# Attention probabilities turned in 32 × 32 squares on VectorE and exchanged through DRAM, instead of transposed on TensorE, in a two-layer diffusion backbone

## The chip, the cores and the metric

The kernel runs on one core of one Trainium2 chip. The metric is the device time of one execution in microseconds (us). Three runs of the kernel before took 1686.21, 1686.81 and 1686.99 us, so its median is 1686.81 us.

## What is computed

Two layers run over 1024 latent tokens of width 1024; 256 context tokens feed the first layer only. Each layer adds a gated branch to x, and a final RMSNorm follows. Layer 0 is windowed attention with 16 query heads, 4 key/value heads, a head size of 128, a window of 128 keys to either side, all 256 context keys and a learned sink in the same softmax. Layer 1 is a Conformer convolution block. What the change touches is the attention:

```python
s_win = jnp.einsum('bqhgd,bkhd->bhgqk', qblk, kw) * scale      # 128 queries, up to 3 blocks of 128 keys
s_win = jnp.where(mask, s_win, -jnp.inf)
s_ctx = jnp.einsum('bqhgd,bchd->bhgqc', qblk, kc) * scale      # 256 context keys
p_ctx, p_win = sink_softmax(sink_l, s_ctx, s_win)
o = (jnp.einsum('bhgqc,bchd->bqhgd', p_ctx, vc)
     + jnp.einsum('bhgqk,bkhd->bqhgd', p_win, vw))
...
y = (o * jax.nn.silu(z)) @ w_out
x = x + gate * y
```

All of it is float32. A product is made of three TensorE matmuls on operands that were split into a high and a low part (high·high, low·high, high·low).

## The kernel before, in words

**Order of the work.** The program is written for the Tile layer, whose scheduler places every engine's instructions by its own simulated times. An engine for which `pin` (line 106) is on keeps the order in which the program names its instructions instead (class InOrder, lines 76 to 91). Since that helper issues everything, all rows of the profile show its line, L89, and one goes by the names of tiles. From line 1260 on, `pin("P")` holds: TensorE works in written order, and VectorE, ScalarE, GpSimd and the SyncE queue (SP), which issues most DMAs, in the scheduler's order.

**The attention loop** (line 1280) has 128 steps, one per head h and block qb of 128 queries. A step writes, for TensorE:

- `scores` (line 1083) of the *next* step: six matmuls into a `pss` bank. VectorE then takes the masked and scaled scores into a page `p_page` with their row minimum, ScalarE takes the exponential, VectorE the reciprocal of the sum, and GpSimd (POOL) multiplies the page by it. `p` then holds 128 queries × 640 keys (512 for the first and the last block of a head): up to five squares of 128 × 128.
- `fill(12)` (line 1070): twelve matmuls of 512 columns out of a queue of projections of later heads (`psg`).
- `pv` (line 1153), the product of probabilities and values into a `pso` bank, when one is due: once per four blocks, 32 times in all; for every other head `pv_shared` (line 1181) adds six short matmuls.
- `transposes` (line 1119) of *this* step's p: five (or four) TensorE transposes into another `pss` bank, from which ScalarE copies the high part `pthi` and VectorE subtracts it for the low part `ptlo`. `pv` reads both. A `pv` is queued at the end of the step whose split closes its four blocks, and runs in the next step behind the fill.

Beside the loop run side works that the loop only advances: `ada_rest` (line 665) loads pieces of 128 KB of the modulation weights (`dww_raw`, `wsum_raw`), which VectorE adds up in `pso`; `low_parts` (line 724) makes the low parts of the two output weights (`low_page`) and stores them in DRAM (`wolA`, `wolC`); the rotary step sends halves through DRAM on ScalarE's queue (`rope_half`); finished heads go to DRAM (`ozd`).

**The output product of layer 1** (`proj_out`, line 1796) runs four passes of eight steps: two token halves, each with two halves of the columns. A step is 24 matmuls of 512 columns, and `ahead` loads the weights (`wo`, `wol`) two steps ahead. At the end of a pass `evac1` (line 1719) runs for each of four row blocks: it names the load of the residual rows (`xr`), adds them, and in the passes for the second column half it also normalises and names the two stores to `out`.

Of the kernel before, what the change touches and what calls it, by code (L numbers as in the profile page):

```python
# [9 lines left out]
F32 = mybir.dt.float32  # L10
# [84 lines left out]
def backbone_kernel(  # L95
# [1023 lines left out]
    def transposes(h, qb):  # L1119
        p = ptile.pop((h, qb))  # L1120
        k0, k1 = max(qb - 1, 0), min(qb + 1, TB - 1)
        nb = k1 - k0 + 1
        tb = ps_s()
        ql = qb % 4
# [7 lines left out]
        tv = tb[:, 0:640].rearrange("p (a b) -> p a b", b=P)  # L1132
        a0, a1 = int(qb == TB - 1), 4 if qb == 0 else 5
        runs = [(a0, a1, slice(ql + 4 * a0, ql + 4 * a1 - 3, 4))]
        if h % 2 == 0 and qb == 3:
            runs = [(1, 5, slice(7, 20, 4)), (0, 1, slice(20, 21))]
        elif h % 2 == 0 and qb == 4:
            runs = [(0, 4, slice(0, 13, 4)), (4, 5, slice(21, 22))]
        for r0, r1, bs in runs:
            anchor_a[:] = [act(pthi[:, bs], tv[:, r0:r1], AF.Copy)]  # L1140
        for r0, r1, bs in runs:
            anchor[:] = [split_lo(V, ptlo[:, bs], tv[:, r0:r1], pthi[:, bs])]

    shared = []

    def pv_mm(o, work):
        for n, (a, b, ps_, os_) in enumerate(work):
            last = n == len(work) - 1
            PE.matmul(o[:, os_], a, pthi[:, ps_], start=n == 0, stop=False)
            PE.matmul(o[:, os_], a, ptlo[:, ps_], start=False, stop=False)  # L1150
            PE.matmul(o[:, os_], b, pthi[:, ps_], start=False, stop=last)

    def pv(h, half):
# [5 lines left out]
        work = [(*(c[:, n, i * P:i * P + P] for n in (2, 3)), slice(4 + 8 * i, 8 + 8 * i), slice(0, 512)) for i in range(2)]  # L1159
        for kb in range(q0, q0 + 4):  # L1160
            qa, qz = max(kb - 1, q0), min(kb + 1, q0 + 3)
            b0 = qa - q0 + 8 * (qa - kb + 1)
            work.append((vh[:, kb], vl[:, kb], slice(b0, b0 + 9 * (qz - qa) + 1, 9), slice((qa - q0) * P, (qz - q0 + 1) * P)))
# [812 lines left out]
```

## Time and profile before

| what | value |
| --- | --- |
| median of three runs | 1686.81 us |
| span of the profiled execution | 1684.8 us |
| between the two | 2.0 us |
| TensorE busy | 1675.0 us, 8436 matmuls |
| VectorE, ScalarE, GpSimd busy | 1116.1, 878.8, 871.0 us |
| DMA | 244.55 MB, mean 145 GB/s |
| attention loop, about | 150 to 750 us of the span |

A row of the timeline gives start and duration in us, the engine, the operation, and the tiles as out<-in; x5 is five instructions with one form in a row. A matmul's printed duration contains the time that it takes to drain, in which the next one already runs, so a matmul's price is the distance between starts. A row of the groups gives count, busy time, mean ns of one, and the idle time before them with what ended it. SPq rows are DMA issues on SP's queue: their duration is that of the issue, not of the transfer. "us to landing" is the median from issue to landing.

### The profile page before, as it was taken

Reading aid. Unit: us, or ns where it says so; the run is one execution under the profiler, and the core shown is the slowest. Engines: PE = TensorE matmul, PEld = TensorE weight load, DVE = VectorE, ACT = ScalarE, POOL = GpSimd, SP = SyncE. Lnnn points to the kernel's source line nnn. Section 1 sums busy time; section 2 is a strip of 40 time slices with the busy share of each in tenths; the row PEclk is TensorE's granted clock in tenths of the full one; section 3 lists DMA queues with packets and bytes.
Section 4 is the critical chain, followed back from the end, with each engine's and each line's share of the span. In section 5 each row is a group of like instructions: output and inputs, shape, how many; then the busy total and the mean of one; then the engine's idle time right before and its main releaser. Section 6 shows DMA issues by size and latency. Waiting matters only on the chain.

```text
span 1684.8 us, 23963 instructions
## 1 busy us (share of the span) xinstructions
PE 1675.0 (99%) x8436; PEld 1413.9 (84%) x8436; DVE 1116.1 (66%) x2131; ACT 878.8 (52%) x1555; POOL 871.0 (52%) x722
## 2 busy tenths in 40 slices
PE   9999999999999999999999999999999999999998
PEld 6888888888888888888888888888888888888886
DVE  5765654566356644566324289999999999868732
ACT  5745543555355543556334365555665654566741
POOL 0256653666366663653001267999898888130400
PEclk9999999999999999999999999999999999999999
DMA  9424443454244443447976522020211202387881
GB/s 387 150 85 153 134 121 95 153 153 141 84 152 144 143 135 98 135 135 251 320 233 228 213 94 91 11 72 17 75 51 51 82 33 80 130 276 241 310 298 50
DMA packets 114776, 244.55 MB, mean 145 GB/s; under 512 B 11626, under 2 KB 36514, under 8 KB 114656
## 3 DMA queue, kind: packets, MB, share of 16 engines
q1 hardware_dynamic: 108576, 233.06, 40.9%
q10 hardware_dynamic: 6080, 9.97, 2.4%
q8 instruction: 66, 1.08, 0.3%
q14 instruction: 54, 0.44, 0.1%
HBM read 190.80 MB, written 41.69 MB: 138 GB/s over the span
## 4 chain that ended last, share of the span: by engine, by line
PE 98%; DVE 0%; DMA 0%; ACT 0%; POOL 0%; issue 0%; ACTq 0%; POOLq 0%
PE psg L89 51%; PE pss L89 26%; PE pso L89 22%; DMA rope_half<-rope_half 0%; POOL rope_half L89 0%; DVE x_page L89 0%; ACT p_page L89 0%; DVE wlo_page L89 0%; ACT pthi L89 0%; ACT rope_half L89 0%; ACT whi_page L89 0%; DVE hf_page L89 0%; DVE hl_page L89 0%; ACT qh_page L89 0%; ACT lhi_page L89 0%
## 5 line engine op out<-in xcount | busy, mean ns | idle before, releaser
L89 POOL TENSOR_TENSOR odd_half<-odd_half,prod_half 128x513 f32<-128x513 f32 (+2 forms) x252 | 314.7, 1257 | 22.6 <-ACT prod_half L89 9.4
L89 POOL TENSOR_TENSOR wlo_page<-wraw_page,whi_page 128x512 fp32r<-128x512 f32 (+1 forms) x104 | 173.0, 1680 | 186.7 <-DVE ql_page L89 72.0
L89 PE MATMUL psg<-hh_page,whi_page 128*128 128x512 f32 x600 | 236.3, 394 | 0.0
L89 PE MATMUL psg<-hl_page,whi_page 128*128 128x512 f32 x600 | 234.4, 391 | 0.0
L89 PE MATMUL psg<-hh_page,wlo_page 128*128 128x512 f32 x600 | 234.0, 390 | 0.0
L89 ACT ACTIVATE prod_half<-ubuf,dww 128x513 f32<-128x513 f32 (+2 forms) x252 | 165.6, 675 | 116.9 <-POOL odd_half L89 113.0
L89 PE MATMUL psg<-h2h_page,whi_page 128*128 128x512 f32 x464 | 181.9, 392 | 0.0
L89 PE MATMUL psg<-h2h_page,wlo_page 128*128 128x512 f32 x464 | 180.6, 389 | 0.0
L89 PE MATMUL psg<-h2l_page,whi_page 128*128 128x512 f32 x464 | 180.6, 389 | 0.0
L89 POOL TENSOR_SCALAR p_page<-p_page,sc 128x640 f32<-128x640 f32 (+1 forms) x128 | 99.6, 779 | 149.5 <-DVE sc L89 131.8
L89 DVE SCALAR_TENSOR_TENSOR pss<-ubuf,dww,pss 128x512 f32<-128x512 f32 (+3 forms) x270 | 172.4, 670 | 0.1
L89 DVE SCALAR_TENSOR_TENSOR pss<-ubuf,wsum,pss 128x512 f32<-128x512 f32 (+3 forms) x270 | 171.7, 671 | 0.2
L89 ACT ACTIVATE p_page<-p_page,sc 128x641 f32<-128x641 f32 (+1 forms) x128 | 102.9, 804 | 98.3 <-DVE sc L89 95.9
L89 ACT ACTIVATE pthi<-pss 128x512 fp32r<-128x512 f32 (+2 forms) x144 | 87.3, 618 | 109.7 <-PE pss L89 99.8
L89 DVE TENSOR_TENSOR ptlo<-pss,pthi 128x512 fp32r<-128x512 f32 (+2 forms) x144 | 101.8, 716 | 61.2 <-ACT pthi L89 59.9
L89 PEld LDWEIGHTS psg<-hh_page,wlo_page 128*128 128x128 f32 x600 | 112.7, 188 | 24.3
L89 PEld LDWEIGHTS psg<-hh_page,whi_page 128*128 128x128 f32 x600 | 112.8, 188 | 19.2 <-ACT hh_page L89 0.3
L89 PEld LDWEIGHTS psg<-hl_page,whi_page 128*128 128x128 f32 x600 | 112.8, 188 | 18.4
L89 ACT ACTIVATE whi_page<-wraw_page 128x1024 fp32r<-128x1024 f32 x88 | 92.6, 1052 | 49.8 <-PE psg L89 21.1
L89 PE MATMUL pso<-h2h_page,whi_page 128*128 128x512 f32 x304 | 118.3, 389 | 0.0
L89 PE MATMUL pso<-h2h_page,wlo_page 128*128 128x512 f32 x304 | 118.3, 389 | 0.0
L89 PE MATMUL pso<-h2l_page,whi_page 128*128 128x512 f32 x304 | 118.3, 389 | 0.0
(262 smaller groups left out, 3992.4 us busy)
## 6 DMA issues: line engine op xcount, KB each, us to landing
wraw_page<-in_k_wconv_dram SPq DMA_DIRECT2D x48, 512.0 KB, 3.3
wraw_page<-in_k_win_dram SPq DMA_DIRECT2D x40, 512.0 KB, 3.6
wo_page<-in_attn_w_out_dram SPq DMA_DIRECT2D x32, 512.0 KB, 6.2
wol_page<-wolA SPq DMA_DIRECT2D x32, 512.0 KB, 8.3
wo_page<-in_conv_w_out_dram SPq DMA_DIRECT2D x32, 512.0 KB, 6.7
wol_page<-wolC SPq DMA_DIRECT2D x32, 512.0 KB, 6.2
rope_half<-rope_half ACTq DMA_DIRECT2D x76, 128.0 KB, 2.4
araw_page<-in_k_ada_dram SPq DMA_DIRECT2D x16, 512.0 KB, 10.1
```

Source lines behind the costliest of these rows:

```text
L89: r = f(*a, **k)
```

## The change

TensorE no longer transposes p. `square_up` lets VectorE turn each 32 × 32 square of p in one instruction into a page `psq`, and SP stores that page in one of four DRAM buffers of 128 × 640 (`psq_610` to `psq_613` below). `land` loads it back with four DMAs, each for 32 partitions in pieces of 640 bytes, so that the squares arrive at their places in a page `pt`: the page then holds p transposed. `split_p` makes `pthi` and `ptlo` from that page rather than from PSUM. The order in the two operands' slots changes with it, and the products read them through explicit address patterns (`pthi_lo`).

The loop is one step deeper for it: `square_up` of the next block behind this step's fill, `land` of the block before at the start of the step, and its `split_p` at the end, so a `pv` runs one step later than it did. And `pin("P")` becomes `pin("PS")`: from the start of the loop to the end of the program SP works in written order too, in the convolution and in both output products as well as in the loop.

```diff
-    def transposes(h, qb):
+    def square_up(h, qb):
         p = ptile.pop((h, qb))
...
-        for kb in range(k1, k0 - 1, -1):
-            at = 2 - 2 * (kb - qb)
-            PE.transpose(tb[:, at * P:(at + 1) * P], p[:, (kb - k0) * P:(kb - k0 + 1) * P], ident)
-        for i in range(2):
-            at = 1 + 2 * i
-            PE.transpose(tb[:, at * P:(at + 1) * P], p[:, (nb + i) * P:(nb + i + 1) * P], ident)
+        nt = 4 if qb in (0, TB - 1) else 5
+        w = nt * P
+        sq = pg.alloc(F32, [1024], "psq")
+        V.transpose(out=sq[:, 0:w].rearrange("p (b t j) -> p t b j", b=4, t=nt),
+                    in_=p[:, 0:w].rearrange("p (t b j) -> p t b j", t=nt, b=4))
         pg.free(p)
...
+        z = squares[(h * TB + qb) % len(squares)]
+        SY.dma_start(out=z[:, 0:w], in_=sq[:, 0:w])
+        pg.free(sq)
+
+    squares = [dr.tile([P, 640], F32, tag=f"psq{i}", name=f"psq{i}") for i in range(4)]
+
+    def land(h, qb):
+        nt = 4 if qb in (0, TB - 1) else 5
+        z = squares[(h * TB + qb) % len(squares)]
+        p = ptile[(h, qb)] = pg.alloc(F32, [1024], "pt")
+        for b in range(4):
+            SY.dma_start(out=p[32 * b:32 * b + 32, 0:nt * P].rearrange("p (a x) -> p a x", a=4),
+                         in_=z[:, b * nt * 32:(b + 1) * nt * 32].rearrange("(a p) x -> p a x", p=32))
...
+    def split_p(h, qb):
+        p = ptile.pop((h, qb))
...
-            anchor_a[:] = [act(pthi[:, bs], tv[:, r0:r1], AF.Copy)]
+            anchor_a[:] = [act(slots(pthi, b0, r1 - r0), pv_[:, r0:r1], AF.Copy)]
...
-            anchor[:] = [split_lo(V, ptlo[:, bs], tv[:, r0:r1], pthi[:, bs])]
+            anchor[:] = [split_lo(V, slots(ptlo, b0, r1 - r0), pv_[:, r0:r1], slots(pthi, b0, r1 - r0))]
+        pg.free(p)
...
-    pin("P")
+    pin("PS")
+    square_up(0, 0)
...
+    landed = deque()
+
+    def split_next():
+        h, qb = landed.popleft()
+        split_p(h, qb)
+        if qb % 4 == 3:
+            pvq.append((h, qb // 4))
...
+        if landed:
+            land(*landed[0])
+        landed.append((h, qb))
         if nxt and not regroup:
             scores(*nxt)
...
             fill(n)
+        if nxt and not regroup:
+            square_up(*nxt)
         if pvq:
             pv(*pvq.popleft())
...
-        transposes(h, qb)
+        if len(landed) > 1:
+            split_next()
...
+    while landed:
+        land(*landed[0])
+        split_next()
```

On TensorE, in the middle of the attention loop, a step before ends its fill (`psg`), transposes p (`ident`), and goes on with the next scores (`kh`, `kl`: keys; `kvc`: context; `qh`, `ql`: queries):

```order
L89 MATMUL psg_1059<-hh_page_449,wlo_page_973 128x512
L89 MATMUL pss_1102<-ident,p_page_1042 128x128 x5
L89 MATMUL pss_1114<-kh_page_610,qh_page_779 128x384
L89 MATMUL pss_1114<-kvc_page_612,qh_page_779 128x256
L89 MATMUL pss_1114<-kl_page_611,qh_page_779 128x384
L89 MATMUL pss_1114<-kvc_page_612,qh_page_779 128x256
L89 MATMUL pss_1114<-kh_page_610,ql_page_780 128x384
L89 MATMUL pss_1114<-kvc_page_612,ql_page_780 128x256
L89 MATMUL psg_1059<-hh_page_499,whi_page_972 128x512
```

The same place now:

```order
L89 MATMUL psg_1914<-hh_page_300,wlo_page_1792 128x512
L89 MATMUL pss_1935<-kh_page_614,qh_page_1485 128x384
L89 MATMUL pss_1935<-kvc_page_616,qh_page_1485 128x256
L89 MATMUL pss_1935<-kl_page_615,qh_page_1485 128x384
L89 MATMUL pss_1935<-kvc_page_616,qh_page_1485 128x256
L89 MATMUL pss_1935<-kh_page_614,ql_page_1486 128x384
L89 MATMUL pss_1935<-kvc_page_616,ql_page_1486 128x256
L89 MATMUL psg_1914<-hh_page_343,whi_page_1791 128x512
```

The row of transposes is gone from every step, and the fill is followed at once by the scores.

On SP's queue in the attention loop, before, only the side works stand (weights loaded as `wraw`, low parts, pieces for `ada_rest`, finished heads):

```order
L89 DMA low_page_3126<-in_attn_w_out_dram 128x2x512
L89 DMA dww_raw<-in_ada_w_dram 128x256
L89 DMA wolA<-low_page_2962 128x1024
L89 DMA wsum_raw<-in_ada_w_dram 128x256
L89 DMA wraw_page_3261<-in_k_win_dram 128x1024
L89 DMA dww_raw<-in_ada_w_dram 128x256
```

A similar stretch of that queue now, two steps long:

```order
L89 DMA psq_613<-psq_page_3435 128x640
L89 DMA wsum_raw<-in_ada_w_dram 128x256
L89 DMA pt_page_3444<-psq_612 32x4x160 x4
L89 DMA psq_610<-psq_page_3480 128x640
L89 DMA dww_raw<-in_ada_w_dram 128x256
L89 DMA pt_page_3489<-psq_613 32x4x160 x4
L89 DMA psq_611<-psq_page_3520 128x640
L89 DMA low_page_3525<-in_attn_w_out_dram 128x2x512
L89 DMA wolA<-low_page_3397 128x1024
```

Each step now adds a store and four loads. The loads of a block (`pt_page_3444<-psq_612`) stand behind the store of the block after it (`psq_613`), and the side works stand among them in written order.

On SP's queue at the end of the second pass of layer 1's output product, before, loads of weights stand before, between and behind the loads of residual rows and the stores of results:

```order
L89 DMA wo_page_15014<-in_conv_w_out_dram 128x2x512
L89 DMA wol_page_15015<-wolC 128x1024
L89 DMA wo_page_15122<-in_conv_w_out_dram 128x2x512
L89 DMA xr_page_15189<-x1d 128x512
L89 DMA out_dram<-x_page_14414 128x512
L89 DMA xr_page_15189<-x1d 128x512
L89 DMA out_dram<-x_page_14821 128x512
L89 DMA wol_page_15051<-wolC 128x1024
L89 DMA wo_page_15254<-in_conv_w_out_dram 128x2x512
```

The same place now, from the first row block's stores on:

```order
L89 DMA out_dram<-x_page_14754 128x512
L89 DMA out_dram<-x_page_15161 128x512
L89 DMA xr_page_15162<-x1d 128x512
L89 DMA out_dram<-x_page_14754 128x512
L89 DMA out_dram<-x_page_15161 128x512
L89 DMA xr_page_15204<-x1d 128x512
L89 DMA out_dram<-x_page_14772 128x512
L89 DMA out_dram<-x_page_15203 128x512
L89 DMA xr_page_15204<-x1d 128x512
L89 DMA out_dram<-x_page_14772 128x512
L89 DMA out_dram<-x_page_15203 128x512
L89 DMA wo_page_15245<-in_conv_w_out_dram 128x2x512
```

All stores and residual loads of the pass stand in row-block order ahead of the next load of weights.

More of the change, by code (lines that the diff above doesn't have):

```diff
@@ L1144, in backbone_kernel, with pthi_lo @@
     shared = []
+    def pthi_lo(b0, step, n):
+        return [bass.AP(t.tensor, t.offset + b0 * P, [t.ap[0], (step * P, n), (1, P)])
+                for t in (pthi[:, 0:22].rearrange("p b n -> p (b n)"), ptlo[:, 0:22].rearrange("p b n -> p (b n)"))]
     def pv_mm(o, work):
@@ L1148, in pv_mm @@
             last = n == len(work) - 1
-            PE.matmul(o[:, os_], a, pthi[:, ps_], start=n == 0, stop=False)
-            PE.matmul(o[:, os_], a, ptlo[:, ps_], start=False, stop=False)
-            PE.matmul(o[:, os_], b, pthi[:, ps_], start=False, stop=last)
+            ph, pl = ps_
+            PE.matmul(o[:, os_], a, ph, start=n == 0, stop=False)
+            PE.matmul(o[:, os_], a, pl, start=False, stop=False)
+            PE.matmul(o[:, os_], b, ph, start=False, stop=last)
     def pv(h, half):
```

50 lines of the change are left out of this document (28 added, 22 removed).

## The prediction

> **What bounds the kernel now.** I read the page's first part and its chain, then the waits of TensorE, and then the stretch of the attention loop by windows.
>
> ```profile
> PE 1675.0 (99%) x8436; PEld 1413.9 (84%) x8436; DVE 1116.1 (66%) x2131; ACT 878.8 (52%) x1555; POOL 871.0 (52%) x722
> PE 98%; DVE 0%; DMA 0%; ACT 0%; POOL 0%; issue 0%; ACTq 0%; POOLq 0%
> ```
>
> TensorE is busy for 99% of the span of 1684.8 us and is 98% of the chain that ended last. All of TensorE's waits together:
>
> ```profile
> PE pss L89 <- DVE zerr_page L89: 2.0, 1, 2.0
> PE pss L89 <- DVE hl_page L89: 0.2, 1, 0.2
> ```
>
> These are 2.2 us, at the program's start. In the attention loop TensorE never waits: whatever the other engines do there is done in time. The window 150 to 750 us, with busy times of TensorE, weight loads, VectorE, ScalarE and GpSimd, then the granted clock, the DMA share and GB/s:
>
> ```profile
> 150.00:750.00 600.00, 599.90 (x3339) 523.21 (x3338) 330.48 (x738) 295.63 (x640) 341.36 (x309) 1.00 0.43 132
> ```
>
> TensorE is busy for 599.90 of 600 us, the other engines for half. So work taken from TensorE shortens the span, until something else comes too late; and what is now in time with no wait has an unknown margin. That margin is what the change spends.
>
> **The change part by part.**
>
> *The transposes leave TensorE.* The group and one place of it on TensorE's timeline:
>
> ```profile
> L89 PE MATMUL pss<-ident,p_page 128*128 128x128 f32 x608 | 87.2, 272 | 0.1
> ```
>
> ```profile
> 403.24 0.71 PE L89 MATMUL pss<-ident,p_page 128*128 128x128 f32 x5
> 403.70 0.42 PE L89 MATMUL pss<-kh_page,qh_page 128*128 128x384 f32 x1
> 403.96 0.28 PE L89 MATMUL pss<-kvc_page,qh_page 128*128 128x256 f32 x1
> 404.08 0.34 PE L89 MATMUL pss<-kl_page,qh_page 128*128 128x384 f32 x1
> 404.26 0.28 PE L89 MATMUL pss<-kvc_page,qh_page 128*128 128x256 f32 x1
> ...
> 404.67 0.40 PE L89 MATMUL psg<-hh_page,whi_page 128*128 128x512 f32 x1
> 404.90 0.39 PE L89 MATMUL psg<-hl_page,whi_page 128*128 128x512 f32 x1
> ```
>
> The group's 272 ns per instruction contains the drain. By distances, five transposes take 403.70 − 403.24 = 0.46 us, and the score matmul behind them takes 0.26 us to the next start where the same shape (`kl_page`) takes 404.26 − 404.08 = 0.18: another 0.08 us that goes with them. A step with five gives 0.54 us; one with four gives 0.54 − 0.09 = 0.45. Each head has six of the first kind and two of the second: 96 × 0.54 + 32 × 0.45 = 66 us. All of it lies on the path, so this term is −66 us (−58 if the 0.08 stays for another reason; no more than −68).
>
> *What remains of the step.* Six scores take 404.67 − 403.70 = 0.97, now 0.9 us; a fill matmul takes 404.90 − 404.67 = 0.23, twelve 2.7. A step of TensorE is then 3.6 us, and at every fourth step a product of probabilities and values (PV) follows.
>
> *The new chain to PV.* The chain before starts with the scores and ends with GpSimd's normalisation. Two samples, scores first, then GpSimd:
>
> ```profile
> 360.00 0.43 PE L89 MATMUL pss<-kh_page,qh_page 128*128 128x384 f32 x1
> ...
> 364.16 0.42 PE L89 MATMUL pss<-kh_page,qh_page 128*128 128x384 f32 x1
> ```
>
> ```profile
> 363.78 0.80 POOL L89 TENSOR_SCALAR p_page<-p_page,sc 128x640 f32<-128x640 f32 x1 [3.51 <-DVE sc L89]
> ...
> 368.33 0.79 POOL L89 TENSOR_SCALAR p_page<-p_page,sc 128x640 f32<-128x640 f32 x1
> ```
>
> From the scores' start to the normalised page: 364.58 − 360.00 = 4.6 and 369.12 − 364.16 = 5.0; I take 4.8 us. The splits that follow before the change:
>
> ```profile
> L89 DVE TENSOR_TENSOR ptlo<-pss,pthi 128x640 fp32r<-128x640 f32 x80 | 65.6, 820 | 28.5 <-ACT pthi L89 28.0
> L89 ACT ACTIVATE pthi<-pss 128x640 fp32r<-128x640 f32 x80 | 56.1, 701 | 46.8 <-PE pss L89 45.9 <-PE pso L89 0.6
> 363.66 0.42 DVE L89 COPY mask_page<-pso 128x256 f32<-128x256 f32 x1
> L89 DVE TENSOR_TENSOR x_page<-x_page,fg_page 128x512 f32<-128x512 f32 x8 | 7.5, 944 | 0.3 <-ACT junk_half L89 0.3
> ```
>
> VectorE's turn of 128 × 640 is not in this trace. I take 0.82 us, the price of VectorE's one pass over the same 640 columns; the ends are 0.42 (a copy of 256 columns) and 1.18 (the dearest full pass, 0.944 us for 512 columns, scaled to 640). Its 128 turns, some 100 us, lie beside 330 of 600 us busy and so cost nothing by themselves, only as delay. The Trainium skill, page "VectorE: DVE Perf Modes", section "The three transpose paths", gives 311 ns for a VectorE transpose of 128 × 128 in bf16, and its "Rules for kernel authors" advise TensorE where PSUM will do as the target; by that figure the turn would be five times 0.311, an estimate of 1.56 us, 0.74 us more in each PV's chain, and the time 28 × 0.74 = 21 us above mine. The trace speaks against that advice so far as 0.54 us per step of the engine that bounds are saved.
>
> Then come SP's issues and the transfers (0.33 to 0.35 us for an issue; landings of transfers of a like size in this loop):
>
> ```profile
> 358.03 0.33 SPq L89 DMA_DIRECT2D wolA<-low_page  x1
> ...
> 363.65 0.35 SPq L89 DMA_DIRECT2D wsum_raw<-in_ada_w_dram  x1
> ```
>
> ```profile
> low_page<-in_conv_w_out_dram SPq DMA_DIRECT2D x16, 512.0 KB, 3.9
> ozd<-oz_half SPq DMA_DIRECT2D x25, 192.0 KB, 2.4
> ```
>
> In SP's written order the loads of a block stand behind the store of the *next* block. So the chain that counts begins with the next block's scores: page normalised 4.8; turn with semaphore 0.92; store issued 0.35; one side load 0.35; three of the four loads issued 1.05; the last lands 2.4; ScalarE's high part with semaphore 0.8; VectorE's low part 0.92. Sum 11.6 us. TensorE reaches that PV three steps after those scores began, 3 × 3.6 = 10.8 us, and the low part is needed 0.23 later: the bare chain is 0.6 us late. Added to it is the waiting for engines that are half busy with other work: about half an instruction each on VectorE (0.4, twice), ScalarE (0.3) and SP (0.1), 1.2 us. I take 1.8 us of wait per PV, with ends of 0 (turn 0.42, nothing in the way) and 3.6 (landing 3.9 as `low_page`, turn 1.18). Of the 32 PVs three have a whole projection of keys and values ahead of them (the regroups), and the last is the loop's end; 28 can wait: 28 × 1.8 = **+50 us** (0 to 100). Behind the waiting PV stand the next scores on TensorE, so the wait is not made up for. The 320 KB of store and 320 KB of load per step are 640 KB in 5 us at most, about the 132 GB/s that the loop moves now: the DMA share goes from 0.43 to about 0.85, which fits but leaves little.
>
> *SP's written order in layer 1's output product.* SP's rows at the end of the second pass and in the last, then the rows that price a row block:
>
> ```profile
> 1599.06 0.38 SPq L89 DMA_DIRECT2D out_dram<-x_page  x1
> ...
> 1601.00 0.44 SPq L89 DMA_DIRECT2D wol_page<-wolC  x1
> ...
> 1638.78 0.80 SPq L89 DMA_DIRECT2D xr_page<-x1d  x2
> 1669.02 12.54 SPq L89 DMA_DIRECT2D out_dram<-x_page  x8
> ```
>
> ```profile
> 1665.58 0.69 DVE L89 TENSOR_TENSOR x_page<-x_page,xr_page 128x512 f32<-128x512 f32 x1
> out_dram<-x_page SPq DMA_DIRECT2D x8, 256.0 KB, 2.6
> L89 ACT ACTIVATE woh_page<-wo_page 128x1024 fp32r<-128x1024 f32 x63 | 66.3, 1056 | 92.7 <-DMA wo_page<-in_conv_w_out_dram 36.3 <-DMA wo_page<-in_attn_w_out_dram 31.5 <-PE psg L89 9.6
> L89 POOL TENSOR_TENSOR x_page<-x_page,xr_page 128x512 f32<-128x512 f32 x4 | 5.8, 1452 | 43.9 <-DVE x_page L89 34.3 <-PE psg L89 4.6 <-DVE ms L89 3.8
> ```
>
> Before, weights are loaded between the stores, and residual rows 27 us before use (1638.78 to 1665.58). In written order a residual load waits behind the stores of the row block ahead of it. A row block then costs, in series: landing 2.6, from the addition to the first store's issue 1669.02 − 1665.58 = 3.44, two issues 0.8: 6.85 us. At the end of the second pass the next weights stand behind all four: the first block's multiplication 0.7 and its 3.44, its stores 0.8, three blocks 20.6 with another 0.76 for each of the two that GpSimd adds (1.45 instead of 0.69), landing 3.9 (as `low_page`) and ScalarE's split 1.06, together 32 us. TensorE has 24 × 0.23 = 5.5 us of work per product step, and until the next weights three quarters of one and two more: 15 us. The hole is 17 us, or 24 where the first block ends as late as now (1599); I take 20. In the last pass stores at 1669.0 for the first block are followed by three serial blocks, 0.8 + 3 × 6.85: the last issue comes at about 1690 instead of 1669.02 + 12.54 = 1681.6, +9. Together **+29 us** (24 to 36). The Trainium skill, page "TensorE: Matmul & The Clock Gate", section "Why this matters for your kernels", says that TensorE's clock falls after idle gaps of over some 3 us; no run here shows that, the granted clock being 1.00 in the window above, and by it the hole would cost some 2 us more.
>
> *The rest of the written order.* In the last head the large weight loads stand ahead of the loads of squares, one 3.9 us landing late or two: +6 (0 to 15).
>
> Sum: 1684.8 − 66 + 50 + 29 + 6 = 1704 us of span, and with the 2.0 us between the span and the median **1706 us**.
>
> **The rivals.**
>
> *A: the squares land in time.* If the wait per PV stays under some 1.1 us (66 − 29 − 6 = 31, divided by 28), the change wins. For it: TensorE never waits now, VectorE, ScalarE and GpSimd are half idle, and the scheduler may put the turn first. Against: the bare chain is already 0.6 us late. With 0.2 us of wait per PV and 3 instead of 6 for the last head: 1684.8 − 66 + 6 + 29 + 3 + 2 = 1659 us. This is the one on the other side.
>
> *B: SP's line of waiting loads.* In written order a load that waits for another engine holds the loads of squares behind it:
>
> ```profile
> SPq L89 <- DVE pso L89: 164.7, 86, 8.3
> ```
>
> Before, SP waited 86 times for VectorE's additions in `pso`, 1.9 us on average, up to 8.3. If such waits or full DMA engines lengthen each chain by 2.2 us more, a PV waits 4 us: 28 × 4 = 112, and 1684.8 − 66 + 112 + 29 + 6 + 2 = 1768 us. For it: these loads stand right between a store and the loads of squares. Against: they are 1.9 us on average and mostly overlap the store's own wait.
>
> *C: the written order does not bind in the output product*, say because loads further ahead cover it: 1684.8 − 66 + 50 + 6 + 2 = 1677 us. Against it stand the rows of the order, in which no weights come between the stores.
>
> That the transposes stay is excluded by the rows of TensorE's order.
>
> **How the numbers follow.** My case has 0.48, its own range 1690 to 1725 (a wait of 1.1 to 2.5 us per PV); A 0.22, C 0.10, B 0.14; the remaining 0.06 lies where the terms cancel within 0.2%, 3.4 us, which is about what a measurement of this kernel can tell from no change. Faster: A and C, 0.32. Same: 0.06. Slower: my case and B, 0.62. The range leaves B out, and a little of A's lower end: 1650 to 1742.
>
> **What would show it.** Right: the group of transposes is gone, TensorE's busy time in the loop falls by 60 to 66 us, TensorE waits about 28 times for `ptlo` or `pthi` with 1 to 2.5 us each, and SP for the next block's `psq_page`; one hole of 17 to 24 us on TensorE near the end of the output product's second pass; the stores of the last pass in series with residual loads. Wrong: no waits for `ptlo` (A), waits of 4 us and more with SP held by `pso` (B), or weights that arrive in time at the pass's end (C). A turn of over 1.2 us, or landings of squares over 4 us, would make the PV term too small.

## The result and the profile after

The changed kernel takes 1993.93 us, the median of four runs (1990.00 to 1995.33); the kernel before took 1686.51 us, the median of four (1685.15 to 1686.99). The ratio is 1.1822, with a 95% interval of 1.1805 to 1.1839: 307 us slower. The forecast was slower too, but by 20 us, with a range that ended at 1742.

The first part of the page after, its clock row and its chain:

```profile
span 1993.5 us, 24171 instructions
PE 1702.4 (85%) x7828; PEld 1405.1 (70%) x7828; DVE 1250.3 (63%) x2283; ACT 901.7 (45%) x1579; POOL 891.6 (45%) x722
PEclk9988889788998888988889999999999999998798
PE 41%; DMA 23%; DVE 13%; POOL 8%; SPq 5%; issue 5%; ACT 4%; ACTq 0%; DVEq 0%; POOLq 0%
```

TensorE has 608 matmuls fewer and yet is busy 27 us longer; it idles for 291 us where it had idled for 10; and its share of the chain that ended last falls from 98% to 41%, with DMA at 23%. The waits of TensorE after:

```profile
PE pso L89 <- ACT pthi L89: 166.7, 26, 11.5
PE pss L89 <- ACT woh_page L89: 24.9, 1, 24.9
PE pso L89 <- DVE ptlo L89: 18.9, 18, 1.8
PE psg L89 <- ACT woh_page L89: 11.5, 2, 9.1
PE pso L89 <- DMA dwr_page<-in_conv_dw_w_dram: 10.7, 1, 10.7
```

The first and third rows are the products of probabilities and values (PV) that wait for the split: 186 us, at 26 places. The second is one hole for weights. Where the time lies is read by windows: the attention loop from the first to the last scores (before 74 to 794, after 73 to 1006), first of before, then of after:

```profile
74.00:794.00 720.00, 719.90 (x4000) 627.08 (x4000) 403.00 (x898) 361.61 (x777) 402.15 (x366) 1.00 0.43 135
```

```profile
73.00:1006.00 933.00, 729.29 (x3406) 610.34 (x3406) 533.28 (x1045) 375.28 (x797) 424.54 (x366) 0.88 0.62 184
1006.00:1210.00 204.00, 183.68 (x808) 149.07 (x808) 64.06 (x128) 66.00 (x95) 17.34 (x21) 0.95 0.65 234
1210.00:1747.00 537.00, 531.47 (x2358) 438.71 (x2356) 506.63 (x817) 314.06 (x448) 424.32 (x311) 0.99 0.20 69
1747.00:1993.00 246.00, 187.24 (x805) 153.37 (x804) 97.98 (x189) 97.39 (x155) 24.28 (x17) 0.87 0.55 192
```

The loop grew by 213 us. TensorE did 594 matmuls fewer in it, was busy for 9 us more and idle for 204. Its granted clock (the figure behind GpSimd's) fell from 1.00 to 0.88. The three stretches behind it (layer 0's output product, the convolution, layer 1's output product) took 177, 529 and 185 us before: with 204, 537 and 246 they grew by 97.

The clock is seen in TensorE's rows around one PV:

```profile
708.26 0.79 PE L89 MATMUL pso<-pthi,kvc_page 128*128 128x512 f32 x1 [5.74 <-ACT pthi L89]
710.19 0.79 PE L89 MATMUL pso<-ptlo,kvc_page 128*128 128x512 f32 x1 [1.14 <-DVE ptlo L89]
...
712.06 0.63 PE L89 MATMUL pso<-pthi,kvc_page 128*128 128x512 f32 x1
712.49 0.41 PE L89 MATMUL pso<-pthi,vh_page 128*128 128x256 f32 x1
...
716.56 0.40 PE L89 MATMUL psg<-hh_page,whi_page 128*128 128x512 f32 x1
716.79 0.40 PE L89 MATMUL psg<-hl_page,whi_page 128*128 128x512 f32 x1
```

After a wait of 5.74 us a matmul of 512 columns takes 712.49 − 712.06 = 0.43 us to the next start; at 716.56 it takes 0.23 again. For some 6 us of its work TensorE runs at little over half its speed. The window of that time has a granted clock of 0.50:

```profile
705.80:716.00 10.20, 6.60 (x20) 5.61 (x21) 6.16 (x10) 3.43 (x8) 6.69 (x6) 0.50 0.59 171
```

The Trainium skill, page "TensorE: Matmul & The Clock Gate", section "Why this matters for your kernels", advises against idle gaps of over some 3 us between matmuls, since the clock falls back to half behind one. The trace agrees: the 26 waits for `pthi` average 6.4 us.

Last, the chain of work that ended last, ahead of that PV (start, us, what; small pieces left out):

```profile
691.31 0.50 DVE pso L89
...
692.17 0.85 DVE psq_page L89
...
693.95 5.74 DMA wolC<-low_page
...
699.78 0.84 DVE psq_page L89
...
704.14 3.24 DMA pt_page<-psq
...
707.49 0.42 ACT pthi L89
...
708.65 1.50 DVE ptlo L89
...
710.19 2.07 PE pso L89 x4
```

Read from the top: VectorE makes a side work's addition in `pso`, and only behind it comes a turn (`psq_page`). The store `wolC<-low_page` takes 5.74 us to land, and the next turn starts when it has: the page that it writes was that `low_page`, by the order in which the pool gave out its pages. Then SP issues the turned page's store, three side works and the four loads of a block that was stored before, the last squares land 3.24 us later, and the two splits follow. Of these 19 us some 4 are work on the probabilities by an engine; the rest is landings, issues and places in queues.

### The profile page after: what moved, and what is told of

It is laid out like the page before. It is cut to its first block, busy times and chain, and to the rows that moved or that the text cites. A ratio compares the mean times of both kernels' runs of the same rounds, so it can differ in the third digit from the quotient of the medians.

```text
span 1993.5 us, 24171 instructions
## 1 busy us (share of the span) xinstructions
PE 1702.4 (85%) x7828; PEld 1405.1 (70%) x7828; DVE 1250.3 (63%) x2283; ACT 901.7 (45%) x1579; POOL 891.6 (45%) x722
## 4 chain that ended last, share of the span: by engine, by line
PE 41%; DMA 23%; DVE 13%; POOL 8%; SPq 5%; issue 5%; ACT 4%; ACTq 0%; DVEq 0%; POOLq 0%
PE psg L89 16%; PE pss L89 13%; PE pso L89 11%; DMA pt_page<-psq 7%; SPq L89 5%; POOL odd_half L89 4%; DVE pss L89 3%; DMA rope_half<-rope_half 3%; DMA psq<-psq_page 3%; DVE ptlo L89 2%; DVE v_page L89 1%; DMA wo_page<-in_conv_w_out_dram 1%; POOL wlo_page L89 1%; DVE psq_page L89 1%; ACT pthi L89 1%
## 5 line engine op out<-in xcount | busy, mean ns | idle before, releaser
L89 DVE TENSOR_TENSOR ptlo<-pt_page,pthi 128x640 fp32r<-128x640 f32 (+3 forms) x168 | 150.5, 911 | 158.3 <-ACT pthi L89 157.4
L89 POOL TENSOR_SCALAR p_page<-p_page,sc 128x640 f32<-128x640 f32 (+1 forms) x128 | 106.3, 831 | 313.2 <-DVE sc L89 243.2
L89 PE MATMUL pso<-pthi,kvc_page 128*128 128x512 f32 x128 | 71.1, 604 | 166.7 <-ACT pthi L89 166.7
L89 ACT ACTIVATE pthi<-pt_page 128x640 fp32r<-128x640 f32 (+3 forms) x168 | 95.5, 586 | 193.8 <-DMA pt_page<-psq 145.5
L89 PEld LDWEIGHTS pso<-pthi,kvc_page 128*128 128x128 f32 x128 | 37.0, 289 | 183.5 <-ACT pthi L89 177.6
L89 DVE STREAM_TRANSPOSE psq_page<-p_page 128x640 f32<-128x640 f32 (+1 forms) x128 | 103.3, 807 | 87.4 <-POOL p_page L89 48.0
L89 PE MATMUL pss<-woh_page,gs_page 128*128 128x512 f32 (+1 forms) x352 | 115.2, 399 | 28.8 <-ACT woh_page L89 24.9
L89 ACT ACTIVATE woh_page<-wo_page 128x1024 fp32r<-128x1024 f32 x63 | 66.6, 1058 | 137.1 <-DMA wo_page<-in_attn_w_out_dram 71.8
```

What stands on the lines that cost most here:

```text
L89: r = f(*a, **k)
```

## The experiments

Each kernel's time is split at the last scores: the loop (first to last scores, from TensorE's rows) and the rest behind it. Each experiment ran once, beside a run of the kernel before (1685.1 to 1687.0 us in all of these). Differences are taken before rounding; those of 11 to 16 us are under 1% of the whole and rest on one run each. "DMA" is the DMA share in the loop's window.

One thing goes for all differences between these kernels. VectorE, ScalarE and GpSimd stand in the scheduler's order (in e11_va and e12_va_deeper GpSimd alone), and the scheduler makes that order anew for each kernel. Of VectorE's some 850 instructions in the loop, turns left out, 785 stand in one common order in e7_no_exchange_free and e14_stores_only, but only 567 in e8_no_turn and e7_no_exchange_free, 637 in e13_to_dram and e10_unread, and 566 in e10_unread and e1_sp_free (the longest sequence of tile names that both traces share). So a difference between two rows is the edit and its new order together; no run holds the order fixed while one part is added.

| kernel | whole, us | loop | rest | clock in the loop | DMA |
| --- | --- | --- | --- | --- | --- |
| before | 1686.5 | 720 | 891 | 1.00 | 0.43 |
| after | 1993.9 | 933 | 988 | 0.88 | 0.62 |
| e1_sp_free | 1854.8 | 873 | 906 | 0.91 | 0.66 |
| e2_before_written | 1789.0 | 731 | 983 | 1.00 | 0.42 |
| e3_no_exchange | 1798.3 | 739 | 984 | 0.97 | 0.41 |
| e4_land_first | 1943.0 | 882 | 985 | | |
| e5_deeper | 1844.8 | 861 | 908 | 0.90 | 0.66 |
| e6_weights_first | 1975.0 | 925 | 974 | | |
| e7_no_exchange_free | 1674.9 | 708 | 892 | 0.98 | 0.44 |
| e8_no_turn | 1641.7 | 675 | 891 | 0.99 | 0.45 |
| e9_own_pages | 1827.6 | 844 | 908 | 0.92 | 0.69 |
| e10_unread | 1777.3 | 804 | 898 | 0.93 | 0.71 |
| e11_va | 2036.3 | 1056 | 905 | 0.84 | 0.54 |
| e12_va_deeper | 2062.8 | 1079 | 908 | | |
| e13_to_dram | 1746.6 | 759 | 912 | 0.96 | 0.73 |
| e14_stores_only | 1684.7 | 719 | 891 | 0.98 | 0.58 |
| e15_cut_store | 1849.9 | 869 | 906 | 0.91 | 0.66 |
| e16_own_deeper | 1805.8 | 820 | 911 | 0.92 | 0.70 |
| e17_land_ahead | 1984.8 | 917 | 993 | | |
| e18_together | 1909.4 | 914 | 920 | | |

### The written order, with and without the exchange

Theory A held SP's written order to be the cause, theory B the exchange's own way through pages, VectorE and ScalarE.

```diff
e1_sp_free (to the changed kernel)
-    pin("PS")
+    pin("P")
e2_before_written (to the kernel before)
-    pin("P")
+    pin("PS")
e3_no_exchange (to the changed kernel)
-        SY.dma_start(out=z[:, 0:w], in_=sq[:, 0:w])
-        pg.free(sq)
+        ptile[(h, qb)] = sq
...
-        p = ptile[(h, qb)] = pg.alloc(F32, [1024], "pt")
-        for b in range(4):
-            SY.dma_start(...)
+        return
...
-        if len(landed) > 1:
-            split_next()
+        split_next()
e4_land_first (to the changed kernel): land(*landed[0]) leaves the head of the step
+        land(h, qb)
         if pvq:
             pv(*pvq.popleft())
```

> The changed kernel with SP's queue placed by the scheduler again, everything else as changed. Theory A (in SP's written order the side loads between the store of the next block and the loads of this block hold the exchange): the stretch from the first to the last scores falls from 933 us to 720 to 770, the output products return to their old lengths, 1660 to 1720 us in all. Theory B (the exchange itself makes a loop through ScalarE, VectorE and the pages, whatever SP's order): the stretch stays above 880 us and only the output products gain, 1860 to 1930 us.

Measured: 1854.8 us, the loop 873. A expected 720 to 770 of the loop, B over 880: the loop lies in neither, 7 us short of B. The rest returns to 906 of 988. The loop regains only 60 of its 213 us, so A is not the main cause there; behind the loop it is.

> The kernel before with SP's queue in written order from the loop on, nothing else. It prices the written order without an exchange. Theory A: the loop loses little, since no PV hangs on SP there, and the last output product loses 30 to 58 us: 1715 to 1790 us. Theory B expects the same of this run; if the loop too grows by over 60 us, then side loads in written order are dear by themselves and A has its mechanism wrong.

Measured: 1789.0 us. Without any exchange the written order costs 102 us: 11 in the loop, 93 behind it. So the written order by itself makes about as much as the rest's 97 us in the changed kernel. The exchange is not wholly free there: with SP placed by the scheduler (e1_sp_free) the rest still lies 15 us above before.

> The changed kernel without the exchange: no store to the squares and no loads from them; the splits read the turned page, one step earlier (so blocks are turned within their squares but not exchanged: part of the transposition is left out). VectorE's turn, SP's written order and the missing transposes stay. If DMA round trip, SP's line or pages held by it are the cause (A and B), the stretch of the loop falls to 650 to 680 us, and the whole to 1700 to 1730. If VectorE's turn and its dearer splits are the cause, the stretch stays above 800 us and the whole above 1850.

Measured: 1798.3 us, the loop 739. Taking the exchange away gives back 194 us of the loop, which lies between the two expectations (650 to 680, and over 800). Yet it stays 19 us above before, though TensorE has no transposes.

> The changed kernel with the four loads of a block named right behind the store of the next block, ahead of the side works of that step; SP stays in written order. Theory A: each chain loses the 5 us that the loads now come behind the store, and the loop's stretch falls by 100 us or more, to 780 to 830, the whole to 1840 to 1890 us. Theory B: what holds the stores themselves (late normalisation, late turn, late pages) stays, and the whole falls by less than 50 us, 1945 to 1990.

Measured: 1943.0 us, the loop 882: loads that stand ahead of the side works save 50 us of the loop. A expected 100 or more, B less than 50 of the whole, which gained 51: side loads ahead of the loads of squares are a part, not the whole.

### What the exchange adds, piece by piece

SP is placed by the scheduler in all of these, so that only the loop changes. e7_no_exchange_free is e3 with `pin("P")`. e8_no_turn leaves the turn out too: `square_up` returns at once, and the split reads p. e14_stores_only adds to e7 the store alone, e10_unread the store and loads into a page that nobody reads, and e13_to_dram sends those loads to another place in DRAM:

```diff
e8_no_turn (to e7_no_exchange_free), in square_up
-        V.transpose(...)
+        return
e14_stores_only (to e7_no_exchange_free)
+        SY.dma_start(out=z[:, 0:w], in_=sq[:, 0:w])
         ptile[(h, qb)] = sq
e10_unread (to e7_no_exchange_free)
+        SY.dma_start(out=z[:, 0:w], in_=sq[:, 0:w])
         ptile[(h, qb)] = sq
...
+        p = pg.alloc(F32, [1024], "pt")
+        for b in range(4):
+            SY.dma_start(...)
+        pg.free(p)
e13_to_dram (to e10_unread)
-        p = pg.alloc(F32, [1024], "pt")
+        p = apart[qb % 2]
...
-        pg.free(p)
```

> No exchange and no turn: the splits read p itself, so the transposition is left out altogether; SP placed by the scheduler. This is the price of TensorE's transposes alone: by the forecast's term the loop's stretch is 720 - 66 = 654 us, the whole 1620 to 1630. The difference to e7_no_exchange_free is what the turn costs; if it is under 10 us, the turn is hidden as the forecast had it, if over 30 us, it is not.

Measured: 1641.7 us, the loop 675. The windows of the loop of e8_no_turn, then of e7_no_exchange_free, e10_unread and e1_sp_free:

```profile
74.00:749.00 675.00, 661.21 (x3403) 568.22 (x3402) 437.15 (x919) 366.33 (x799) 419.69 (x366) 0.99 0.45 144
```

```profile
73.00:781.00 708.00, 674.13 (x3404) 576.40 (x3403) 520.43 (x1045) 368.84 (x802) 424.96 (x365) 0.98 0.44 137
```

```profile
74.00:878.00 804.00, 704.78 (x3405) 591.40 (x3404) 517.94 (x1047) 369.90 (x801) 421.65 (x365) 0.93 0.71 217
```

```profile
74.00:947.00 873.00, 720.10 (x3406) 605.04 (x3405) 522.54 (x1046) 369.12 (x799) 424.67 (x366) 0.91 0.66 200
```

With the same count of matmuls TensorE's busy time climbs from 661 to 720 us as its clock falls, and its idle time from 14 to 153.

> No exchange, as in e3_no_exchange (part of the transposition is left out), and SP placed by the scheduler. If the written order alone made that loop's stretch 739 instead of 720 - 66 = 654 us, it comes to 650 to 680 us and the whole to 1620 to 1650. If VectorE's turn and the splits out of SBUF cost time by themselves, the stretch stays between 700 and 740 us and the whole between 1670 and 1710.

Measured: 1674.9 us, the loop 708: the turn, with the page that it takes and the order that comes with it, costs 33 us, though it adds 83 us of VectorE's time to an engine that was half idle. This kernel and the two beside it (e8, e14) are the only ones not slower than the kernel before, and all three leave out a part of the work.

> As e10_unread without the four loads: only the store of 320 KB per block is added to e7_no_exchange_free (the exchange is left out). If landings of loads in pages cost the most, the stretch is near 708, at most 735 us, the whole 1675 to 1705. If the store (which holds the psq page until it has landed) costs half of the 96 us, it is 750 to 765 and the whole 1715 to 1735.

Measured: 719, that is 11 us for the stores.

> As e10_unread, but the four loads per block go from the squares to another place in DRAM instead of into a page: same count, same pieces of 640 bytes, no page held (part of the transposition is left out, as in e10_unread). If the 96 us that e10_unread lies above e7_no_exchange_free are pages held by landings, the loop's stretch falls from 804 to 720 to 750 us and the whole to 1685 to 1720; if they are the traffic or SP's issues, it stays at 785 or more, the whole at 1755 or more.

Measured: 759, that is 40 us for the loads' issues and traffic, and 45 below e10_unread. It lies between the two expectations, 9 us above the 720 to 750 of "pages" and 26 below the 785 of "traffic or issues": both have a part.

> SP placed by the scheduler; the squares are stored and loaded as in the change, but the loaded page is read by nobody: the splits read the turned page as in e7_no_exchange_free (part of the transposition is left out). All traffic, issues and pages are there; only the dependence of split on landing is gone. If that dependence makes the loop (splits that wait for a landing hold ScalarE and VectorE, and with them the next softmax), the stretch comes to 705 to 740 us, near the 708 without an exchange, and the whole to 1670 to 1710. If traffic or pages make it, the stretch stays over 800 us and the whole over 1780.

Measured: 804, just over the 800 that stood for traffic or pages. The 96 us above e7 are then 11 for the stores, 40 for the loads as such, and 45 that go when the loads no longer land in pages. ScalarE's first touch of a new page for scores speaks for pages that stay taken until a load has landed; its group between 120 and 940 us in e13_to_dram, e10_unread and e1_sp_free:

```profile
L89 ACT ACTIVATE p_page<-nsink 128x1 f32<-128x1 f32 x117 | 22.6, 195 | 65.8 <-DMA psq<-psq_page 17.9 <-DVE psq_page L89 15.1 <-DMA rope_half<-rope_half 9.1
```

```profile
L89 ACT ACTIVATE p_page<-nsink 128x1 f32<-128x1 f32 x118 | 22.4, 196 | 110.9 <-DVE psq_page L89 41.1 <-DMA pt_page<-psq 27.3 <-DMA psq<-psq_page 16.5
```

```profile
L89 ACT ACTIVATE p_page<-nsink 128x1 f32<-128x1 f32 x118 | 23.0, 197 | 142.7 <-DMA psq<-psq_page 52.1 <-DVE psq_page L89 47.4 <-DMA rope_half<-rope_half 11.6
```

ScalarE idles ahead of these tiny copies for 66, 111 and 143 us, and most of what ends the idle time in the last two are the turns and transfers that held the page. From e13 to e10 it is 45 us more, with `pt_page<-psq` new among the causes. But the loads' destination changed as well as the page, and that was not tried apart. From e10 to e1 the split waits for its landing and stands a step later, and the loop takes another 69 us.

### What makes the landings late

```diff
e5_deeper (to e1_sp_free)
-        if landed:
+        if len(landed) > 1:
             land(*landed[0])
...
-        if len(landed) > 1:
+        if len(landed) > 2:
             split_next()
e9_own_pages (to e1_sp_free)
-    pg = Pages(pgpool, 45, "page", 1024)
+    pg = Pages(pgpool, 44, "page", 1024)
+    sqp = Pages(hfpool, 2, "sqp", 640)
-        sq = pg.alloc(F32, [1024], "psq")
+        sq = sqp.alloc(F32, None, "psq")
...
-        pg.free(sq)
+        sqp.free(sq)
e11_va (to the changed kernel)
-    pin("PS")
+    pin("PVA")
e15_cut_store (to e1_sp_free)
+        z = squares[0 if n == 1 else 1 + n % 3]       # store
+        z = squares[0]                                # loads
e17_land_ahead (to the changed kernel)
         if landed:
             land(*landed[0])
+        if i and (h % 4 or qb):
+            square_up(h, qb)
```

e16_own_deeper is e5 with the edit of e9, e12_va_deeper e11 with that of e5. All three with a step more have six squares in DRAM instead of four; e11 and e12 return to `pin("P")` behind the loop.

> SP placed by the scheduler as in e1_sp_free, and the loads and splits of a block one step later still (with six squares in DRAM). If the loop is held by latency alone (the chain from scores to split is longer than the steps allowed for it), another step of 3.6 us takes most of the 4.2 us of wait per PV away: the loop's stretch falls from 873 us to 740 to 790, the whole to 1720 to 1775 us. If it is held by a rate (splits that wait on ScalarE and VectorE for landings hold the next softmax, and pages that come free late), a step more changes little: the stretch stays over 840 us, the whole over 1820.

Measured: 861 for 873. A whole step more for the way through DRAM gives 12 us: it is not a fixed latency that the loop's depth could hide.

> SP placed by the scheduler as in e1_sp_free, and the turned squares in two buffers of their own instead of pages of the common pool, so no page of the next scores is one whose store is still under way. If pages that come free late make the loop slow, its stretch falls from 873 us to 800 or less and the whole from 1855 to under 1785 us; if not, it stays over 850, the whole over 1830.

Measured: 844, 28 us better; between the two readings. Pages are a part.

> e9_own_pages and e5_deeper together: SP placed by the scheduler, turned squares in buffers of their own, loads and splits one step later. If depth was of no use in e5_deeper because pages ran short, the two together free the loop: a stretch under 780 us, under 1755 in all. If the gains of 28 and 12 us only add up, it is 825 to 840 us and the whole 1805 to 1820: another rate holds it.

Measured: 820. Together they give 52 us, a little more than the sum of 40; a third of the 153 us by which that loop lies above before.

> As e1_sp_free, with ScalarE and VectorE in written order in the loop: there the next block's softmax and turn always stand ahead of the split of the block that has to land. If the scheduler's places for the splits (too early for the real landing) hold the softmax, the stretch falls from 873 us to under 800 and the whole under 1785 us. If the loop is held otherwise, it stays over 850 us.

Measured: 1056, 184 us worse. In written order ScalarE and VectorE do worse still, so nothing here shows the scheduler's places for splits and turns to be the fault; only this one other order was tried.

> As e11_va, and loads and splits a step later as in e5_deeper. With written order on ScalarE and VectorE and one more step of 3.6 us for the way through DRAM, theory B's loop is open: no split waits for a landing, the stretch comes to 690 to 740 us and the whole to 1660 to 1715. If it stays over 800 us, then neither place nor depth is the cause, and the rate of something else (pages, SP's issues) is.

Measured: 1079. This reading of theory B falls with it.

> As e1_sp_free, but every block loads the squares of the first full block, so no load waits for its own block's store (the probabilities are wrong for it; traffic, issues, pages and the wait of the split for the landing are all there). If the dependence costs time as a loop or chain through softmax, turn, store and landing, cutting it here gives back the same 69 us as cutting it at the split did: a stretch of 790 to 820 us, 1765 to 1795 in all. If only the wait of ScalarE for a landing counts, the stretch stays over 850 us.

Measured: 869. That is over the 850 of the second expectation. A load that need not wait for its own store is no help, so the way through softmax, turn, store and landing of one block is not what closes the loop.

> The changed kernel, SP in written order, with turn and store of a block named behind the loads of the block before it instead of ahead of them. On SP a block's loads then no longer wait for the next block's softmax and turn, only for their own store. If that wait is what makes the landings late, the loop's stretch falls from 933 us to 860 or less and the whole under 1920. If the landings are late through side loads or pages, it stays over 910 us, 1970 in all; slower than 933 if SP, which now waits for each store's landing of 2.4 us, becomes the rate.

Measured: 917 for 933. The next block's turn ahead of the loads, on which the forecast's chain was built, is worth 15 us, a fourteenth of the loss. SP now waits for the stores' landings instead, and for something that is there in both; its waits between 125 and 1005 us after, then in e17_land_ahead:

```profile
SPq L89 <- DVE psq_page L89: 126.3, 54, 6.8
SPq L89 <- DVE oz_half L89: 104.2, 21, 16.2
```

```profile
SPq L89 <- DMA psq<-psq_page: 138.1, 81, 5.1
SPq L89 <- DVE oz_half L89: 111.6, 22, 17.7
```

`oz_half` is a PV's own result on its way to DRAM. Its store stands in SP's order ahead of the loads for the next PV: SP waits up to 16 us for a PV that itself is late. That this closes the loop through TensorE is argued from the rows and was not tried. Nor was another rival: with SP placed by the scheduler (e1_sp_free) the side works still stand in SP's queue, and there SP waits most for VectorE's additions in `pso`; between 125 and 945 us:

```profile
SPq L89 <- DVE pso L89: 78.3, 52, 6.4
```

No run takes the side works off that queue.

### The order behind the loop, and all together

```diff
e6_weights_first (to the changed kernel)
+                ahead(i, EA + 3, 0, 0)
                 for b in range(4):
                     evac1(s, b, acc[b])
e18_together (to e17_land_ahead): the edit of e9, and behind the loop
+    pin("P")
```

> The changed kernel, SP in written order, but in layer 1's output product the weights of the next three steps are named ahead of a pass's residual loads and stores. If TensorE's one wait of 24.9 us for the split of weights comes from weights that stand behind four row blocks' stores, it falls to under 5 us and the product's stretch from 227.5 us to 195 to 205, the whole from 1994 to 1960 to 1970 us. If it comes from elsewhere (pages, a slow landing), nothing moves by more than 5 us.

Measured: 1975.0 us; the product, from 1747 us after to TensorE's last matmul, takes 208 us instead of 227. That is more than the expected 195 to 205. Its waits for weights:

```profile
PE pss L89 <- ACT woh_page L89: 10.6, 2, 9.0
PE psg L89 <- ACT woh_page L89: 8.0, 1, 8.0
```

The single hole of 24.9 us has shrunk to 9.0, where under 5 were expected; the other, of 8.0, stands in the changed kernel too, with 9.1. So the stores ahead of the weights made most of the hole, and three steps ahead don't quite cover it.

> As e17_land_ahead, with turned squares in buffers of their own as in e9_own_pages and SP placed by the scheduler from the loop's end on. The rest after the loop returns to 891 us (988 in the changed kernel); with 28 us from the pages the whole comes to 1780 to 1830. Under 1686 us it would beat the kernel before, which needs a loop of 720 us or less: not expected by any theory, since e10_unread, without any wait for a landing, has 804.

Measured: 1909.4 us, the loop 914, where 1780 to 1830 in all were expected. Own buffers gave nothing here beside e17 (917), where they had given 28 us with SP placed by the scheduler. The best whole exchange is e16_own_deeper with 1805.8 us, 7% above the kernel before.

## Why the prediction was wrong, point by point

**The transposes leave TensorE: −66 forecast.** e8_no_turn prices this alone. TensorE's busy time falls from 1675.0 to 1615.6, by 59 us; the time by 45. The 0.54 us per step were about right (the near end of −58 comes to −56 by its own terms, 66 less 128 × 0.08); what the forecast left out is what comes late next. The three largest rows of waits in its loop:

```profile
PE pss L89 <- POOL ql_page L89: 7.9, 6, 1.9
PE psg L89 <- DVE zs_page L89: 2.5, 1, 2.5
PE pss L89 <- ACT qh_page L89: 2.3, 2, 1.9
```

With shorter steps, and in the order that the scheduler made for them, the rotated queries of the next head come too late from GpSimd and ScalarE, where nothing had waited.

**The turn: 0.82 us forecast, "nothing by itself".** The price was right:

```profile
L89 DVE STREAM_TRANSPOSE psq_page<-p_page 128x640 f32<-128x640 f32 x96 | 80.6, 840 | 52.9 <-POOL p_page L89 22.1 <-POOL wlo_page L89 12.6 <-DMA wolA<-low_page 7.9
```

0.84 us for 640 columns. The Trainium skill's figure of 311 ns, page "VectorE: DVE Perf Modes", section "The three transpose paths", taken five times, had given an estimate of 1.56; here the measurement decides. That VectorE's idle half would hide the turn was wrong: 33 us (e8 to e7). The same page's advice in "Rules for kernel authors", TensorE for 128 × 128 where PSUM will do as the target, was right for this kernel.

**The wait per PV: 1.8 us forecast, +50 (0 to 100).** This is the step that failed. Measured are 186 us of waits for the splits, 7.1 per waiting PV, four times the forecast and twice its upper end. The transfers were near their price of 2.4 us (medians over the program of after):

```profile
psq<-psq_page SPq DMA_DIRECT2D x96, 320.0 KB, 2.5
pt_page<-psq SPq DMA_DIRECT2D x384, 80.0 KB, 2.9
```

Neither the turn (0.84 us) nor the landing of the squares (2.9) passed the 1.2 and 4 us that the forecast had named as signs. What was mis-sized is "the waiting for engines that are half busy", 1.2 us in all. Medians over the 128 blocks, worked out from the trace's rows, in us from a block's own scores: page normalised 7.0 (4.8 forecast), turned 9.0, store issued 10.0, first load issued 19.2, landed 24.1 (where the trace has the landing), low part ready 27.1. Counted in the same way the forecast was one step of 3.6, the chain's 11.6 and the 1.2: 16.4 us. TensorE allows four steps, 14.4 us. Between store and loads lie 9 us where one step of 3.6 was meant: there the block's loads stand in SP's line. An average of half an instruction per hop assumes that a queue moves on; in the chain above VectorE's next turn stood still for the 5.74 us of a landing.

**The clock: not in the sum of the loop.** It is the term that was left out. From e8 to after TensorE is busy for 87 us more (1615.6 to 1702.4) with the same 7828 matmuls, 68 of these us in the loop (661 to 729). In e8, whose longest wait in the loop is 2.5 us, the loop's clock is 0.99; with waits of 6.4 us on average it is 0.88. So waits of the forecast's size would have cost little of this.

**DMA: "fits but leaves little".** The share was to rise to 0.85 and rose to 0.62, since the loop became longer; with the loop faster it is 0.71 (e10). Traffic and issues cost 51 us (e7 to e13, by way of e14), a cost for which the sum had no term.

**The written order behind the loop: +29 and +6 forecast, +97 measured.** The two places named were right: one hole of 24.9 us (17 to 24 forecast) and a tail that ends 11.5 us later (9 forecast). Their own ends, 17 + 9 and 24 + 9, make 26 to 33, not the 24 to 36 of the forecast. What was missed, since the +6 stood for the loop's last head: 27 us in layer 0's output product, where TensorE waited 10.7 us for a small load (`dwr_page`) that stood in line; 8 in the convolution, with a wait of 5.4 us; and in the last product further waits of 15 us and 10 us of slower clock (187 us busy where it was 177).

**The rivals.** A (the squares land in time) and C (the order doesn't bind) are refuted by the rows above. B named the right kind: loads of squares that stand in SP's line, and pages and transfers that lengthen each chain; e4_land_first shows 50 us for the line. But SP was held less by `pso` in the loop than before (36 us instead of 163); it was held by `psq_page` and `oz_half`. B was priced at 4 us of wait instead of 7, without the clock, and given 0.14.

So the 258 us of the loop from e8 to after are, in this order of adding: turn 33, stores 11, loads 40, pages held by them 45 (the pages as argued above), splits that wait for the landing 69, SP's written order 60. Each figure is an edit together with the order that the scheduler made for it, as said above, and the sequence of adding matters: without an exchange the written order costs 31 (e7 to e3), not 60. Open is what keeps the landings late in e1_sp_free: of the 153 us above before, depth and pages explain 52, and the own store and another place of the splits explained nothing. Theory A fell as the main cause in the loop. Of B it stands that the exchange is dear whatever SP's order; the loop through ScalarE, VectorE and the pages that it named was not shown.

## What to carry to other kernels

Work taken from the engine that bounds is worth only as much as the new path's queues allow: ask at each hop for the longest wait that the queue's head can meet, such as a landing, and don't price it at half an instruction alone, and add the clock for every wait of several us on TensorE. (That such prices add up to the right sum is not shown here.) A queue put in written order is put there for the rest of the program: read its order to the end, and ask for each row what it waits for and who stands behind it. And do the cheap split first: a kernel without the turn and one without the exchange tell what the change can bring at most (here 45 us, and 11 with the turn), before any tuning of the path.

## What the runs showed of the hardware

Other transfers land later beside those of the exchange, though the mean DMA share is far from full, and not in step with that share. From issue to landing between 200 and 700 us, in e7_no_exchange_free (share 0.44 in the loop), then in e14_stores_only (0.58) and e10_unread (0.71):

```profile
wraw_page<-in_k_win_dram SPq DMA_DIRECT2D x28, 512.0 KB, 3.6
rope_half<-rope_half ACTq DMA_DIRECT2D x54, 128.0 KB, 2.6
```

```profile
wraw_page<-in_k_win_dram SPq DMA_DIRECT2D x27, 512.0 KB, 5.4
rope_half<-rope_half ACTq DMA_DIRECT2D x54, 128.0 KB, 4.1
```

```profile
wraw_page<-in_k_win_dram SPq DMA_DIRECT2D x25, 512.0 KB, 4.0
rope_half<-rope_half ACTq DMA_DIRECT2D x49, 128.0 KB, 3.6
```

With the stores alone each takes half as long again; with stores and loads, at the higher share, less than that. Why is not shown. And a block's four loads alone hold SP for 2 us, more than half of a 3.6 us step, a row of SP's timeline after:

```profile
702.76 1.97 SPq L89 DMA_DIRECT2D pt_page<-psq  x4
```
